# A decoder layer on one core: eight triangular matrices inverted together instead of four and four

## The chip, the cores and the metric

The kernel runs on one core of a Trainium2 chip. The core has TensorE (matrix products, with a queue that loads weights ahead), VectorE (DVE), ScalarE (ACT), GpSimd (POOL) and SyncE (SP, which issues most of the transfers). The metric is the device time of one run in microseconds; lower is better.

## The reference

One layer of a decoder with 256 positions of 1024 features. A norm is followed by one projection whose columns go to two mixers:

- softmax attention with 8 heads of 64 (one block, a relative bias, normed queries and keys), with a gate;
- a gated delta rule with 4 heads of 128. Queries, keys and values pass a convolution of width 4. The 256 positions of a head are cut into chunks of 64, and in each chunk a lower triangular system is solved:

```
g = cumsum(g, axis=-1)                       # per chunk of 64
decay = where(incl, exp(g_i - g_j), 0)
lmat = where(strict, (k*beta) @ k.T * decay, 0);  amat = lmat + eye(C)
u = triangular_solve(amat, v * beta)
w = triangular_solve(amat, k * beta * exp(g))
def step(state, xs):                         # over the chunks
    v_new = u_i - w_i @ state
    o_i = q_i @ state + a_i @ v_new
    state = state * gl_i + k_i.T @ v_new
```

Both outputs are gated, joined, projected back to 1024 and added to the input.

## The kernel before, in words

**Large products.** The weights stream in as chunks of 512 KB (8 smaller `z`, 12 `d`, 16 `a`, 8 `o`). Each is split into a high part (`wh`, a cast on ScalarE, L195) and the rest (`wl`, a subtraction on VectorE, L196), and every product runs as three products of 256 columns (L256 to L258, L747 to L749, L836 to L838). The `z` chunks give the gates, `d` the queries, keys and values of the delta rule, `a` those of the attention and its gate, `o` is the output projection.

**The order.** `products()` emits the large products in steps of six and yields after each; `advance()` then counts a slot (`now`) and lets every other stream (`bias`, `norm`, `gates`, `prep`, `base`, `scan`, `heads`, `pair`) whose slot has come emit its next step. The table `AT` gives the slot of each step of each stream; a slot that has passed means the next one. If `products()` itself must wait (for the bank of PSUM or, in the output projection, for a head that isn't done), slots go by without a large product. TensorE runs in exactly the order in which its instructions are emitted. The other engines' order is set by a planner at build time, which lets what is ready go ahead of what was emitted earlier, with streams preferred to the splits of weights.

**The delta rule.** The kernel uses chunks of 128, two for each head, so 8 triangular matrices (index `u`). `prep(0)` makes those of heads 0 and 1, `prep(2)` those of heads 2 and 3: transposes of keys and queries (L438), products of them (L462), then the scaled triangle `LT` (L466) and transposes of values (L478). `base` inverts: the 16x16 blocks on the diagonal by substitution on VectorE, 15 steps of a multiply (L507) and a subtraction (L509), then `levels` puts them together to 32, 64 and 128 with small products on 32- or 64-row tiles of TensorE (L529; L535 and L537; L552; L558 to L560; L568; L574), with an eviction to SBUF after each. The result is `MT`. `scan` then runs the chunks of a head in five dependent steps (L589; L595 and L596; L610 and L611; L618; L622), norms the output with a power on GpSimd, transposes it (L634) and writes `yh` and `yl`, high part and rest (L635, L636). `scan` of head 2 waits for head 0 and that of head 3 for head 1.

Before, `base(0)` with `levels(0)` does the four matrices of heads 0 and 1 as soon as `prep(0)` has them, and `base(1)` those of heads 2 and 3 after `prep(2)`; each set of levels uses one bank.

**Attention.** `heads4` norms and transposes queries and keys (L663); `pair` does two heads: logits (L689), softmax on VectorE and ScalarE (L696, L123, L700, L707), transposes (L712), product with the values (L723, L725).

**Output.** `OUTS` orders the output chunks. The second chunk needs heads 0 and 1 of the scan, the fifth needs attention heads 4 to 7, the seventh needs scan heads 2 and 3.

**Others that move.** `bias` has one product (L381) whose result is copied (L384) and sent through memory to spread the relative bias. `norm` ends with L297, whose copy (`rbc`) each convolution (L403, L405, L407) reads. `gates` makes the decays: its small steps end with `g` (L345), which L352, L353 and L363 read.

Of the kernel before, what the change touches and what calls it, by code (L numbers as in the profile page):

```python
# [11 lines left out]
ALU = mybir.AluOpType  # L12
AX = mybir.AxisListType

P = 128
# [5 lines left out]
DH = 4  # L21
# [6 lines left out]
C_ID, C_MN, C_U, C_ND = range(4)  # L28
# [6 lines left out]
LD, LS, PRI, REP, MTL, BDK = 7, 4, 100, 16, 1, 14  # L35
OUTS = ((0, 2), (0, 0), (1, 2), (1, 0), (0, 3), (1, 3), (0, 1), (1, 1))
AT = {
    ("attention", 0): 88, ("attention", 1): 97, ("attention", 2): 128, ("attention", 3): 117, ("attention", 4): 120,
# [3 lines left out]
    ("base1", 8): 124, ("bias", 0): 0, ("bias", 1): 6, ("bias", 2): 43, ("gates", 0): 29, ("gates", 1): 35,  # L42
# [13 lines left out]
}  # L56
SEGS = (2, 0, 1, 3)
W_NORM, W_BA, W_PREP, W_BASE, W_LV, W_SC, W_Y, W_QK, W_SM, W_PT, W_HD, NP = 7, 16, 4, 34, 2, 3, 5, 6, 2, 2, 3, 2
# [3 lines left out]
def tile_hymba_layer(ctx: ExitStack, tc: tile.TileContext, xt, wz, wdn, wat, wout, rb, cst, oneh, out):  # L62
# [11 lines left out]
    def new(shape, name, dt=F32):  # L74
        return cp.tile(shape, dt, name=name, tag=name)
# [20 lines left out]
    def start(name, gen, wait=1):  # L96
        streams.append([gen, AT.get((name, 0), now[0] + wait), name, 0])
# [137 lines left out]
    cvd = new([P, DH, 2], "cvd")  # L235
    M = new([64, 8, 64], "M")
    MT = new([P, 8, P], "MT")
    Mts = [new([P, 4, 32], f"Mt{g}") for g in range(2)]
    for t in (M, MT):
        POOL.memset(t, 0.0)  # L240

    def basis():
        for t in Mts:
            nc.gpsimd.dma_start(t, cst[:, C_ND, :])

    if not MTL:
        basis()
# [175 lines left out]
    def prep(hp, n, ps):  # L423
# [60 lines left out]

    def base(gq):
        us = slice(4 * gq, 4 * gq + 4)
        pk = rot([P, 16, 4], f"pk{gq}", "pk")
        for q in range(4):  # L490
            r = slice(32 * q, 32 * q + 32)

            DVE.scalar_tensor_tensor(out=pk[r].rearrange("p i u -> p u i"), in0=LT[r, us, 32 * q + 16:32 * q + 32],
                                     scalar=cs2[r, 0:1], in1=LT[r, us, 32 * q:32 * q + 16], op0=ALU.mult, op1=ALU.add)
        Lb = rot([P, 16, 32], f"Lb{gq}", "Lb", 1)
        DVE.transpose(Lb, pk.unsqueeze(3).to_broadcast([P, 16, 4, 8]))
        Mt = Mts[gq]
        tm = rot([P, 4, 16], f"tm{gq}", "tm")
# [12 lines left out]
        Mp = rot([P, 4, 4, 8], f"Mp{gq}", "Mp")  # L511
        DVE.transpose(Mp.rearrange("p u c g -> p c u g"), Mt)
        Mp = Mp.rearrange("p u c g -> p u (c g)")
        for q in range(4):
            r = slice(32 * q, 32 * q + 32)
            DVE.transpose(MT[r, us, r], Mp[r])
        yield W_BASE
        yield from levels(gq, Mp)


    def levels(gq, Mp):
        us = slice(4 * gq, 4 * gq + 4)
        uu = range(4 * gq, 4 * gq + 4)
        b = yield from grab()
        b32 = b.rearrange("p (z u i) -> p z u i", z=4, i=32)
# [4 lines left out]
        X16 = rot([P, 4, 16], f"X16{gq}", "X16")  # L530
        ACT.mul(X16, b32[:, 2, :, 0:16], cs2[:, 0:1])
        yield W_LV
        for i, u in enumerate(uu):
            for q, r in enumerate(qs):
                PE.matmul(b32[r, 3, i, 0:16], lhsT=MT[r, u, r], rhs=X16[r, i, :], start=True, stop=True)  # L535
            for q, r in enumerate(qs):
                PE.matmul(b32[32 * q:32 * q + 16, 3, i, 16:32], lhsT=X16[r, i, :], rhs=MT[r, u, 32 * q + 16:32 * q + 32],  # L537
                          start=True, stop=True)
        DVE.tensor_tensor(out=Mp[:, :, 0:16], in0=Mp[:, :, 0:16], in1=b32[:, 3, :, 0:16], op=ALU.subtract)
        for q in range(4):  # L540
            r = slice(32 * q, 32 * q + 16)
            o = MT[r, us, 32 * q + 16:32 * q + 32]
            if q % 2:
                ACT.mul(o, b32[r, 3, :, 16:32], -1.0)
            else:
                DVE.tensor_scalar(out=o, in0=b32[r, 3, :, 16:32], scalar1=-1.0, scalar2=None, op0=ALU.mult)
        for q in range(2):
            POOL.tensor_copy(M[qs[q], us, qs[q]], Mp[qs[q]])
        yield W_LV
        for i, u in enumerate(uu):  # L550
            for r, c in ((q0, q1), (q2, q3)):
                PE.matmul(b32[c, 0, i, :], lhsT=LT[r, u, c], rhs=Mp[r, i, :], start=True, stop=True)  # L552
        X32 = rot([P, 4, 32], f"X32{gq}", "X32")
        ACT.copy(X32[q1], b32[q1, 0])
        DVE.tensor_copy(X32[q3], b32[q3, 0])
        yield W_LV
        for i, u in enumerate(uu):
            PE.matmul(b32[q1, 1, i, :], lhsT=MT[q1, u, q1], rhs=X32[q1, i, :], start=True, stop=True)  # L558
            PE.matmul(b32[q2, 1, i, :], lhsT=X32[q3, i, :], rhs=MT[q3, u, q3], start=True, stop=True)
            PE.matmul(b32[q0, 1, i, :], lhsT=X32[q1, i, :], rhs=MT[q1, u, q1], start=True, stop=True)  # L560
        DVE.tensor_scalar(out=M[q1, us, q0], in0=b32[q1, 1], scalar1=-1.0, scalar2=None, op0=ALU.mult)
        ACT.mul(MT[q2, us, q3], b32[q2, 1], -1.0)
        ACT.mul(MT[q0, us, q1], b32[q0, 1], -1.0)
        yield W_LV
        b64 = b.rearrange("p (z u i) -> p z u i", z=2, i=64)
        for i, u in enumerate(uu):
            for c in (q2, q3):
                PE.matmul(b64[c, 1, i, :], lhsT=LT[0:64, u, c], rhs=M[:, u, :], start=True, stop=True)  # L568
        X64 = rot([P, 4, 64], f"X64{gq}", "k2", 4)
        ACT.copy(X64[64:128], b64[64:128, 1])  # L570
        yield W_LV
        for i, u in enumerate(uu):
            for c, o in ((q0, 0), (q1, 32)):
                PE.matmul(b64[c, 0, i, :], lhsT=X64[64:128, i, o:o + 32], rhs=MT[64:128, u, 64:128], start=True, stop=True)  # L574
# [361 lines left out]
```

## Time and profile before

| | us |
|---|---|
| median of 3 runs (lowest, highest) | 165.27 (165.08, 165.45) |
| the profiled execution | 166.0 |
| its span, first to last instruction | 164.1 |
| TensorE busy in the span | 156.8 (96%) |
| VectorE busy | 130.3 (79%) |
| ScalarE busy | 103.1 (63%) |
| GpSimd busy | 19.8 (12%) |

The profile is of one execution. A product of TensorE has one or two records (a float32 product of two passes has two). Products overlap, so a busy TensorE is read by the time from the start of one to the start of the next. "Idle before" is what the engine stood still ahead of an instruction, with the instruction that it waited for.

### The profile page before, as it was taken

Reading aid. Unit: us, or ns where it says so; the run is one execution under the profiler, and the core shown is the slowest. Engines: PE = TensorE matmul, PEld = TensorE weight load, DVE = VectorE, ACT = ScalarE, POOL = GpSimd, SP = SyncE. Lnnn points to the kernel's source line nnn. Section 1 sums busy time; section 2 is a strip of 40 time slices with the busy share of each in tenths; the row PEclk is TensorE's granted clock in tenths of the full one; section 3 lists DMA queues with packets and bytes.
Section 4 is the critical chain, followed back from the end, with each engine's and each line's share of the span. In section 5 each row is a group of like instructions: output and inputs, shape, how many; then the busy total and the mean of one; then the engine's idle time right before and its main releaser. Section 6 shows DMA issues by size and latency. Waiting matters only on the chain.

```text
span 164.1 us, 4034 instructions
## 1 busy us (share of the span) xinstructions
PE 156.8 (96%) x1548; PEld 148.3 (90%) x1548; DVE 130.3 (79%) x381; ACT 103.1 (63%) x244; POOL 19.8 (12%) x29
## 2 busy tenths in 40 slices
PE   7999899999999999999999999999999979999990
PEld 7869899999999999999999989989988858999990
DVE  2569859999598999999999999987676997356261
ACT  5769497539988558787636695655657885343100
POOL 7200410000002000031230001042220010003000
PEclk9999999999999999999999999999999999999999
DMA  5999888899965327574344434434312300000033
GB/s 148 270 365 355 248 262 222 248 179 192 339 206 209 128 80 213 223 216 172 122 138 135 132 123 134 128 132 132 116 51 93 128 0 4 0 0 0 4 128 128
DMA packets 9930, 25.01 MB, mean 152 GB/s; under 512 B 1165, under 2 KB 3981, under 8 KB 9912
## 3 DMA queue, kind: packets, MB, share of 16 engines
q1 hardware_dynamic: 9208, 23.66, 46.6%
q10 hardware_dynamic: 576, 0.92, 1.5%
q8 instruction: 12, 0.20, 0.5%
q0 software_dynamic: 128, 0.18, 0.4%
q14 instruction: 6, 0.05, 0.1%
HBM read 23.52 MB, written 1.25 MB: 151 GB/s over the span
## 4 chain that ended last, share of the span: by engine, by line
PE 70%; DVE 13%; ACT 6%; DMA 3%; issue 2%; SPq 2%; POOL 1%; DVEq 0%
PE ps L256 8%; PE ps L257 7%; PE ps L258 7%; PE ps L748 6%; PE ps L749 6%; PE ps L747 6%; PE ps L836 4%; PE ps L838 4%; PE ps L837 4%; DVE wl_d L196 3%; DMA px<-xt 3%; PE ps L462 2%; DVE cv L407 2%; PE ps L689 1%; PE ps L712 1%
## 5 line engine op out<-in xcount | busy, mean ns | idle before, releaser
L256 PE MATMUL ps<-wh_a,xh 128*128 128x256 f32 x96 | 28.5, 297 | 0.0
L747 PE MATMUL ps<-xh,wh_d 128*128 128x256 f32 x96 | 27.8, 289 | 0.0
L748 PE MATMUL ps<-xl,wh_d 128*128 128x256 f32 x96 | 26.8, 280 | 0.0
L749 PE MATMUL ps<-xh,wl_d 128*128 128x256 f32 x96 | 26.8, 279 | 0.0
L257 PE MATMUL ps<-wh_a,xl 128*128 128x256 f32 x96 | 26.7, 279 | 0.0
L258 PE MATMUL ps<-wl_a,xh 128*128 128x256 f32 x96 | 26.7, 279 | 0.0
L195 ACT CAST wh_a<-wr_a 128x1024 fp32r<-128x1024 f32 x16 | 16.8, 1049 | 7.2 <-PE ps L748 3.7
L196 DVE TENSOR_TENSOR wl_a<-wr_a,wh_a 128x1024 fp32r<-128x1024 f32 x16 | 19.4, 1215 | 0.7 <-ACT wh_a L195 0.6
L256 PEld LDWEIGHTS ps<-wh_a,xh 128*128 128x128 f32 x96 | 18.1, 188 | 0.7 <-issue 0.5
L836 PE MATMUL ps<-yh,wh_o 128*128 128x256 f32 x64 | 18.7, 292 | 0.0
L257 PEld LDWEIGHTS ps<-wh_a,xl 128*128 128x128 f32 x96 | 18.1, 188 | 0.1
L258 PEld LDWEIGHTS ps<-wl_a,xh 128*128 128x128 f32 x96 | 18.1, 189 | 0.0
L748 PEld LDWEIGHTS ps<-xl,wh_d 128*128 128x128 f32 x96 | 18.1, 188 | 0.1
L747 PEld LDWEIGHTS ps<-xh,wh_d 128*128 128x128 f32 x96 | 18.0, 188 | 0.1
L407 DVE SCALAR_TENSOR_TENSOR cv<-un,px,cv 128x255 f32<-128x255 f32 (+2 forms) x36 | 16.4, 475 | 2.0 <-ACT cv L405 2.0
L749 PEld LDWEIGHTS ps<-xh,wl_d 128*128 128x128 f32 x96 | 18.0, 187 | 0.0
L837 PE MATMUL ps<-yl,wh_o 128*128 128x256 f32 x64 | 17.9, 280 | 0.0
L838 PE MATMUL ps<-yh,wl_o 128*128 128x256 f32 x64 | 17.9, 279 | 0.0
L196 DVE TENSOR_TENSOR wl_d<-wr_d,wh_d 128x1024 fp32r<-128x1024 f32 x12 | 14.6, 1214 | 1.2 <-ACT wh_d L195 1.1
L195 ACT CAST wh_d<-wr_d 128x1024 fp32r<-128x1024 f32 x12 | 12.6, 1052 | 2.4 <-PE ps L748 1.9
L196 DVE TENSOR_TENSOR wl_o<-wr_o,wh_o 128x1024 fp32r<-128x1024 f32 x8 | 9.8, 1221 | 3.6 <-ACT wh_o L195 3.6
L836 PEld LDWEIGHTS ps<-yh,wh_o 128*128 128x128 f32 x64 | 12.0, 188 | 0.5 <-issue 0.3
(210 smaller groups left out, 406.7 us busy)
## 6 DMA issues: line engine op xcount, KB each, us to landing
wr_a<-wat SPq DMA_DIRECT2D x16, 512.0 KB, 3.3
wr_d<-wdn SPq DMA_DIRECT2D x12, 512.0 KB, 5.6
wr_o<-wout SPq DMA_DIRECT2D x8, 512.0 KB, 3.3
wr_z<-wz SPq DMA_DIRECT2D x7, 260.0 KB, 5.8
T<-bd SPq DMA_DIRECT2D x8, 128.0 KB, 5.8
px<-xt SPq DMA_DIRECT2D x7, 128.0 KB, 4.9
out_t<-ot ACTq DMA_DIRECT2D x3, 256.0 KB, 2.4
cs<-cst SPq DMA_DIRECT2D x1, 192.0 KB, 4.9
```

What stands on the lines that cost most here:

```text
L195: ACT.copy(h[:, r], raw[:, r])
L196: eng.tensor_tensor(out=l[:, r], in0=raw[:, r], in1=h[:, r].bitcast(F32), op=ALU.subtract)
L256: PE.matmul(ps, lhsT=xa, rhs=wh[:, cols], start=first, stop=False)
L257: PE.matmul(ps, lhsT=xb, rhs=wh[:, cols], start=False, stop=False)
L258: PE.matmul(ps, lhsT=xa, rhs=wl[:, cols], start=False, stop=last)
L407: DVE.scalar_tensor_tensor(out=a[:, 3 - j:], in0=src[:, 0:S - 3 + j], scalar=pr[:, o + j:o + j + 1], in1=a[:, 3 - j:], op0=ALU.mult, op1=A ...
L747: PE.matmul(ps, lhsT=w[0][:, wk], rhs=xh[:, k, :], start=first, stop=False)
L748: PE.matmul(ps, lhsT=w[0][:, wk], rhs=xl[:, k, :], start=False, stop=False)
L749: PE.matmul(ps, lhsT=w[1][:, wk], rhs=xh[:, k, :], start=False, stop=last)
L836: PE.matmul(ps, lhsT=w[0][:, o], rhs=yh[:, k, :], start=(first and j == 0 and (m % 2 == 0 or alone)), stop=False)
L837: PE.matmul(ps, lhsT=w[0][:, o], rhs=yl[:, k, :], start=False, stop=False)
L838: PE.matmul(ps, lhsT=w[1][:, o], rhs=yh[:, k, :], start=False, stop=(last and j == 1 and (m % 2 == 1 or alone)))
```

## The change

All eight matrices are inverted in one `base`, started when `prep(2)` has its triangles, with instructions twice as wide, and one pass of `levels` over eight matrices with two banks; the last eviction is shared by VectorE and ScalarE. All four `scan` streams are then started at once (2 and 3 still wait for 0 and 1). The slots of all streams are set anew.

```diff
 AT = {
-    ("base0", 0): 40, ("base0", 1): 100, ("base0", 2): 107, ("base0", 3): 112, ("base0", 4): 105, ("base0", 5): 116,
-    ("base0", 6): 104, ("base0", 7): 107, ("base0", 8): 119, ("base1", 0): 93, ("base1", 1): 117, ("base1", 2): 107,
-    ("base1", 3): 121, ("base1", 4): 125, ("base1", 5): 118, ("base1", 6): 116, ("base1", 7): 122,
-    ("base1", 8): 124, ("bias", 0): 0, ("bias", 1): 6, ("bias", 2): 43, ("gates", 0): 29, ("gates", 1): 35,
-    ("gates", 2): 29, ("gates", 3): 49, ("heads00", 0): 82, ("heads00", 1): 96, ("heads01", 0): 120,
-    ("heads01", 1): 120, ("heads10", 0): 95, ("heads10", 1): 98, ("heads11", 0): 125, ("heads11", 1): 127,
-    ("norm", 0): 13, ("norm", 1): 14, ("norm", 2): 18, ("pair0", 0): 101, ("pair0", 1): 112, ("pair0", 2): 118,
-    ("pair1", 0): 93, ("pair1", 1): 107, ("pair1", 2): 118, ("pair2", 0): 111, ("pair2", 1): 148, ("pair2", 2): 151,
-    ("pair3", 0): 144, ("pair3", 1): 187, ("pair3", 2): 193, ("prep0", 0): 44, ("prep0", 1): 30, ("prep0", 2): 46,
...
+    ("attention", 0): 17, ("attention", 1): 45, ("attention", 2): 15, ("attention", 3): 5, ("attention", 4): 38,
+    ("base", 0): 15, ("base", 1): 121, ("base", 2): 127, ("base", 3): 128, ("base", 4): 129, ("base", 5): 130,
+    ("base", 6): 131, ("bias", 0): 15, ("bias", 1): 20, ("bias", 2): 49, ("gates", 0): 27, ("gates", 1): 27,
+    ("gates", 2): 29, ("gates", 3): 30, ("heads00", 0): 11, ("heads00", 1): 92, ("heads01", 0): 35,
+    ("heads01", 1): 121, ("heads10", 0): 14, ("heads10", 1): 102, ("heads11", 0): 1, ("heads11", 1): 128,
+    ("norm", 0): 7, ("norm", 1): 14, ("norm", 2): 28, ("pair0", 0): 105, ("pair0", 1): 120, ("pair0", 2): 121,
+    ("pair1", 0): 105, ("pair1", 1): 120, ("pair1", 2): 121, ("pair2", 0): 130, ("pair2", 1): 134,
+    ("pair2", 2): 138, ("pair3", 0): 136, ("pair3", 1): 140, ("pair3", 2): 142, ("prep0", 0): 53, ("prep0", 1): 54,
+    ("prep0", 2): 55, ("prep0", 3): 36, ("prep0", 4): 58, ("prep0", 5): 59, ("prep0", 6): 60, ("prep0", 7): 61,
+    ("prep0", 8): 38, ("prep2", 0): 30, ("prep2", 1): 67, ("prep2", 2): 76, ("prep2", 3): 15, ("prep2", 4): 78,
+    ("prep2", 5): 79, ("prep2", 6): 80, ("prep2", 7): 81, ("prep2", 8): 24, ("scan0", 0): 132, ("scan0", 1): 133,
+    ("scan0", 2): 134, ("scan0", 3): 136, ("scan0", 4): 134, ("scan0", 5): 140, ("scan1", 0): 132,
+    ("scan1", 1): 133, ("scan1", 2): 134, ("scan1", 3): 136, ("scan1", 4): 137, ("scan1", 5): 142,
+    ("scan2", 0): 141, ("scan2", 1): 143, ("scan2", 2): 144, ("scan2", 3): 147, ("scan2", 4): 147,
+    ("scan2", 5): 159, ("scan3", 0): 142, ("scan3", 1): 143, ("scan3", 2): 144, ("scan3", 3): 147,
+    ("scan3", 4): 148, ("scan3", 5): 157,
 }
...
-    Mts = [new([P, 4, 32], f"Mt{g}") for g in range(2)]
+    Mt = new([P, 320], "Mt")
...
-        start(f"base{hp // 2}", base(hp // 2))
+        if hp == 2:
+            start("base", base())
...
-    def base(gq):
+    def base():
...
-            t = ap(tm, 0, (32, 2), (16, nc_), (1, w))
-            m = ap(Mt, r + 1, (80, 2), (32, nc_), (1, w))
-            SUB.tensor_tensor(out=t, in0=ap(Lb, 32 * (r + 1) + r, (16, 2), (0, nc_), (32, w)),
-                               in1=ap(Mt, r, (80, 2), (32, nc_), (0, w)), op=ALU.mult)
+            t = ap(tm, 0, (32, 4), (16, nc_), (1, w))
+            m = ap(Mt, r + 1, (80, 4), (32, nc_), (1, w))
+            SUB.tensor_tensor(out=t, in0=ap(Lb, 64 * (r + 1) + r, (16, 4), (0, nc_), (64, w)),
+                              in1=ap(Mt, r, (80, 4), (32, nc_), (0, w)), op=ALU.mult)
             SUB.tensor_tensor(out=m, in0=m, in1=t, op=ALU.subtract)
...
-    def levels(gq, Mp):
-        us = slice(4 * gq, 4 * gq + 4)
-        uu = range(4 * gq, 4 * gq + 4)
-        b = yield from grab()
+    def levels(Mp):
+        while len(free) <= keep[0] + 1:
+            yield
+        ba, bb = free.pop(0), free.pop(0)
...
-        for i, u in enumerate(uu):
+        for u in range(8):
             for r in qs:
-                PE.matmul(b32[r, 2, i, 0:16], lhsT=LT[r, u, r], rhs=Mp[r, i, 0:16], start=True, stop=True)
+                PE.matmul(a32[r, 0, u, 0:16], lhsT=LT[r, u, r], rhs=Mp[r, u, 0:16], start=True, stop=True)
...
-        ACT.mul(MT[0:64, us, 64:128], b64[0:64, 0], -1.0)
-        free.append(b)
-        yield W_LV
-        start(f"scan{2 * gq}", scan(2 * gq))
-        yield 1
-        start(f"scan{2 * gq + 1}", scan(2 * gq + 1))
+        DVE.tensor_scalar(out=MT[0:64, 0:4, 64:128], in0=b64[0:64, 0:4], scalar1=-1.0, scalar2=None, op0=ALU.mult)
+        ACT.mul(MT[0:64, 4:8, 64:128], b64[0:64, 4:8], -1.0)
+        free.extend((ba, bb))
+        for h in range(DH):
+            start(f"scan{h}", scan(h))
```

## Rows read from the trace of the kernel before

**Rows 1.** Windows: length, busy us of PE, PEld, DVE, ACT, POOL; granted clock; transfers.

```profile
18.00:125.00 107.00, 106.86 (x1174) 102.45 (x1173) 95.04 (x280) 73.02 (x176) 13.68 (x14) 1.00 0.57 171
...
128.90:137.80 8.90, 7.73 (x61) 5.66 (x59) 8.14 (x34) 7.14 (x22) 0.69 (x1) 1.00 0.15 52
137.80:160.00 22.20, 22.20 (x190) 22.08 (x188) 11.26 (x31) 5.79 (x12) 1.36 (x2) 1.00 0.07 25
```

**Rows 2.** The waits of TensorE's weight loads: us in total, times, longest.

```profile
PEld ps L712 <- DVE pb L707: 1.9, 3, 1.1
```

**Rows 3.** Groups by line: count, busy us, mean ns of one, idle before.

```profile
L507 DVE TENSOR_TENSOR tm<-Lb,Mt 128x28 f32<-128x28 f32 (+10 forms) x30 | 5.5, 184 | 0.4
L509 DVE TENSOR_TENSOR Mt<-Mt,tm 128x28 f32<-128x28 f32 (+10 forms) x30 | 5.3, 175 | 0.5
...
L635 ACT ACTIVATE yh<-ps,px 128x256 fp32r<-128x256 f32 x4 | 1.9, 469 | 3.5 <-PE ps L634 3.5
...
L636 DVE SCALAR_TENSOR_TENSOR yl<-ps,px,yh 128x256 fp32r<-128x256 f32 x4 | 1.9, 482 | 2.4 <-ACT yh L635 2.4
```

**Rows 4.** TensorE in order of time, around two stages of levels: start, us.

```profile
88.78 0.28 PE L258 MATMUL ps<-wl_a,xh 128*128 128x256 f32 x1
88.99 0.44 PE L529 MATMUL ps<-Mp,LT 32*32 32x16 f32 x32
89.36 0.39 PE L256 MATMUL ps<-wh_a,xh 128*128 128x256 f32 x1
89.58 0.28 PE L257 MATMUL ps<-wh_a,xl 128*128 128x256 f32 x1
...
107.95 0.44 PE L529 MATMUL ps<-Mp,LT 32*32 32x16 f32 x32
108.32 0.39 PE L256 MATMUL ps<-wh_a,xh 128*128 128x256 f32 x1
```

**Rows 5.** TensorE in order of time, around the bias product.

```profile
10.18 0.29 PE L258 MATMUL ps<-wl_z,xh 128*128 128x264 f32 x1
10.40 0.81 PE L381 MATMUL ps<-T,rbt 33*8 33x384 f32 x2
...
11.36 0.36 PE L257 MATMUL ps<-wh_z,xl 128*128 128x256 f32 x1
11.95 0.39 PE L258 MATMUL ps<-wl_z,xh 128*128 128x256 f32 x1 [0.23 <-DVE wl_z L196]
```

**Rows 6.** TensorE in order of time: the norm's broadcast and the first gate product.

```profile
21.00 0.60 PE L297 MATMUL ps<-cs,rtok 128*128 128x128 f32 x4
...
33.47 0.28 PE L352 MATMUL ps<-g,cs 128*128 128x8 f32 x2
```

**Rows 7.** VectorE in order of time: the end of the gate steps.

```profile
30.55 0.16 DVE L345 TENSOR_TENSOR g<-ln,eal 128x8 f32<-128x8 f32 x1
```

**Rows 8.** The chain that ended last, from 124 to 140 us: start, us, what.

```profile
124.99 0.91 PE ps L689 x8
...
130.60 1.13 DVE wl_o L196
...
136.17 0.22 PE ps L610 x2
...
137.06 0.58 PE ps L723 x4
137.64 0.22 PE ps L725 x4
```

**Rows 9.** TensorE in order of time, in the stretch without large products.

```profile
129.69 0.93 PE L689 MATMUL ps<-kT,qT 64*128 64x128 f32 x8
...
134.68 0.81 PE L712 MATMUL ps<-cs,pb 128*128 128x128 f32 x4 [0.91 <-DVE pb L707]
135.73 0.44 PE L712 MATMUL ps<-cs,pb 128*128 128x128 f32 x2 [0.24 <-DVE pb L707]
...
137.79 0.39 PE L836 MATMUL ps<-yh,wh_o 128*128 128x256 f32 x1
```

More of the change, by code (lines that the diff above doesn't have):

```diff
@@ L242, in basis @@
     def basis():
-        for t in Mts:
-            nc.gpsimd.dma_start(t, cst[:, C_ND, :])
+        for g in range(2):
+            nc.gpsimd.dma_start(Mt[:, 160 * g:160 * g + P], cst[:, C_ND, :])
     if not MTL:
@@ L482, in prep @@
             yield 1
-    def base(gq):
-        us = slice(4 * gq, 4 * gq + 4)
-        pk = rot([P, 16, 4], f"pk{gq}", "pk")
+    def base():
+        pk = rot([P, 16, 8], "pk", "pk", 1)
         for q in range(4):
             r = slice(32 * q, 32 * q + 32)
[L493 to L498, printed above, removed]
+            DVE.scalar_tensor_tensor(out=pk[r].rearrange("p i u -> p u i"), in0=LT[r, :, 32 * q + 16:32 * q + 32],
+                                     scalar=cs2[r, 0:1], in1=LT[r, :, 32 * q:32 * q + 16], op0=ALU.mult, op1=ALU.add)
+        Lb = rot([P, 16, 64], "Lb", "Lb", 1)
+        DVE.transpose(Lb, pk.unsqueeze(3).to_broadcast([P, 16, 8, 8]))
+        tm = rot([P, 8, 16], "tm", "tm", 1)
         def ap(t, offset, *dims):
@@ L515, in base @@
             r = slice(32 * q, 32 * q + 32)
-            DVE.transpose(MT[r, us, r], Mp[r])
+            DVE.transpose(MT[r, :, r], Mp[r])
         yield W_BASE
-        yield from levels(gq, Mp)
-    def levels(gq, Mp):
-        us = slice(4 * gq, 4 * gq + 4)
-        uu = range(4 * gq, 4 * gq + 4)
-        b = yield from grab()
-        b32 = b.rearrange("p (z u i) -> p z u i", z=4, i=32)
+        yield from levels(Mp)
+    def levels(Mp):
+        while len(free) <= keep[0] + 1:
+            yield
+        ba, bb = free.pop(0), free.pop(0)
@@ L532, in levels @@
+        X16 = rot([P, 8, 16], "X16", "X16", 1)
+        ACT.mul(X16, a32[:, 0, :, 0:16], cs2[:, 0:1])
         yield W_LV
-        for i, u in enumerate(uu):
+        for u in range(8):
+            for r in qs:
+                PE.matmul(a32[r, 1, u, 0:16], lhsT=MT[r, u, r], rhs=X16[r, u, :], start=True, stop=True)
             for q, r in enumerate(qs):
-                PE.matmul(b32[r, 3, i, 0:16], lhsT=MT[r, u, r], rhs=X16[r, i, :], start=True, stop=True)
-            for q, r in enumerate(qs):
-                PE.matmul(b32[32 * q:32 * q + 16, 3, i, 16:32], lhsT=X16[r, i, :], rhs=MT[r, u, 32 * q + 16:32 * q + 32],
+                PE.matmul(a32[32 * q:32 * q + 16, 1, u, 16:32], lhsT=X16[r, u, :], rhs=MT[r, u, 32 * q + 16:32 * q + 32],
@@ L538, in levels @@
                           start=True, stop=True)
-        DVE.tensor_tensor(out=Mp[:, :, 0:16], in0=Mp[:, :, 0:16], in1=b32[:, 3, :, 0:16], op=ALU.subtract)
+        DVE.tensor_tensor(out=Mp[:, :, 0:16], in0=Mp[:, :, 0:16], in1=a32[:, 1, :, 0:16], op=ALU.subtract)
         for q in range(4):
             r = slice(32 * q, 32 * q + 16)
-            o = MT[r, us, 32 * q + 16:32 * q + 32]
+            o = MT[r, :, 32 * q + 16:32 * q + 32]
             if q % 2:
-                ACT.mul(o, b32[r, 3, :, 16:32], -1.0)
+                ACT.mul(o, a32[r, 1, :, 16:32], -1.0)
@@ L545, in levels @@
             else:
-                DVE.tensor_scalar(out=o, in0=b32[r, 3, :, 16:32], scalar1=-1.0, scalar2=None, op0=ALU.mult)
+                DVE.tensor_scalar(out=o, in0=a32[r, 1, :, 16:32], scalar1=-1.0, scalar2=None, op0=ALU.mult)
         for q in range(2):
-            POOL.tensor_copy(M[qs[q], us, qs[q]], Mp[qs[q]])
+            POOL.tensor_copy(M[qs[q], :, qs[q]], Mp[qs[q]])
         yield W_LV
-        for i, u in enumerate(uu):
+        for u in range(8):
             for r, c in ((q0, q1), (q2, q3)):
-                PE.matmul(b32[c, 0, i, :], lhsT=LT[r, u, c], rhs=Mp[r, i, :], start=True, stop=True)
@@ L553, in levels @@
-        X32 = rot([P, 4, 32], f"X32{gq}", "X32")
+                PE.matmul(b32[c, 0, u, :], lhsT=LT[r, u, c], rhs=Mp[r, u, :], start=True, stop=True)
+        X32 = rot([P, 8, 32], "X32", "X32", 1)
         ACT.copy(X32[q1], b32[q1, 0])
@@ L556, in levels @@
         yield W_LV
[L557 to L562, printed above, removed]
@@ L563, in levels @@
-        ACT.mul(MT[q0, us, q1], b32[q0, 1], -1.0)
+        for u in range(8):
+            PE.matmul(b32[q1, 1, u, :], lhsT=MT[q1, u, q1], rhs=X32[q1, u, :], start=True, stop=True)
+            PE.matmul(b32[q2, 1, u, :], lhsT=X32[q3, u, :], rhs=MT[q3, u, q3], start=True, stop=True)
+            PE.matmul(b32[q0, 1, u, :], lhsT=X32[q1, u, :], rhs=MT[q1, u, q1], start=True, stop=True)
+        DVE.tensor_scalar(out=M[q1, :, q0], in0=b32[q1, 1], scalar1=-1.0, scalar2=None, op0=ALU.mult)
+        ACT.mul(MT[q2, :, q3], b32[q2, 1], -1.0)
@@ L564, in levels @@
+        ACT.mul(MT[q0, :, q1], b32[q0, 1], -1.0)
         yield W_LV
-        b64 = b.rearrange("p (z u i) -> p z u i", z=2, i=64)
-        for i, u in enumerate(uu):
+        a64, b64 = (b.rearrange("p (u i) -> p u i", i=64) for b in (ba, bb))
+        for u in range(8):
             for c in (q2, q3):
-                PE.matmul(b64[c, 1, i, :], lhsT=LT[0:64, u, c], rhs=M[:, u, :], start=True, stop=True)
-        X64 = rot([P, 4, 64], f"X64{gq}", "k2", 4)
-        ACT.copy(X64[64:128], b64[64:128, 1])
+                PE.matmul(a64[c, u, :], lhsT=LT[0:64, u, c], rhs=M[:, u, :], start=True, stop=True)
@@ L571, in levels @@
+        X64 = rot([P, 8, 64], "X64", "k2", 4)
+        ACT.copy(X64[64:128], a64[64:128])
         yield W_LV
-        for i, u in enumerate(uu):
+        for u in range(8):
             for c, o in ((q0, 0), (q1, 32)):
-                PE.matmul(b64[c, 0, i, :], lhsT=X64[64:128, i, o:o + 32], rhs=MT[64:128, u, 64:128], start=True, stop=True)
-        ACT.mul(MT[0:64, us, 64:128], b64[0:64, 0], -1.0)
-        free.append(b)
-        yield W_LV
-        start(f"scan{2 * gq}", scan(2 * gq))
-        yield 1
```

11 lines of the change are left out of this document (6 added, 5 removed), and 8 rows, old and new, of the table AT.

## The prediction

> **What bounds the kernel now.** I read the windows first. From 18 to 125 us TensorE is busy for 106.86 of 107.00 us, and from 137.8 us to the end of its work for all of 22.20; between them lies a stretch of 8.9 us in which it works for 7.73 [rows 1]. So almost nothing is left idle: the order of TensorE's instructions is written out by hand through the slots, TensorE runs through it without a gap, and its own work sets the end. VectorE is busy for 95.04 of the same 107.00 us and ScalarE for 73.02, but neither holds TensorE up there. The waits say the same: the transposes of the softmax weights (L712) waited three times, 1.9 us in sum, for the VectorE step ahead of them (L707) [rows 2]; two of the three lie in the stretch of 8.9 us. A change to this kernel therefore counts by three things only: how long TensorE's own instructions take, what is put into its dense stretches, and how long it stands still where the order leaves it no large product to do. Work taken from VectorE or ScalarE counts for nothing by itself.
>
> **Part 1: half the substitution instructions.** Before, 30 multiplies (L507, mean 184 ns) and 30 subtractions (L509, mean 175 ns) [rows 3] are 5.5 + 5.3 = 10.8 us of VectorE. After, 15 + 15 of twice the width. A width of 128x28 costs little more than the smallest ones in these groups, so I take 200 to 250 ns for each, 6 to 7.5 us in all. The packing, the transposes and the evictions halve in number too. VectorE saves 5 to 6 us and TensorE nothing, since in the dense stretch [rows 1] it does not wait for VectorE. In the slot table the one substitution starts at slot 81 and its first product (L529) is due at slot 121: 40 slots of about 0.7 us, which covers the 7 us several times.
>
> **Part 2: one pass of levels.** The number of small products is the same (168, two records each). What changes is how often TensorE goes over from large products to 32- or 64-row tiles and back. The rows show the price [rows 4]: a large product follows the one before by 0.12 us, the first small one starts 0.21 us after the last large one (88.78 to 88.99), the 32 records take 0.37 us, and the second large product starts 0.22 us after the first (89.36 to 89.58). So each visit costs 0.09 + 0.10 = 0.19 us beside its content. Where one small stage follows another, as at 107.95, the second adds its 0.37 us alone. I count visits by walking the two slot tables, each slot's stream steps in order and then one step of large products. Before, up to the stretch at 128.9 us, 13: slots 100, 101, 107, 112, 113, 116, 117, 118, 121, 125, 126, 127, 129. After, 7: slots 105, 121 and 127 to 131. Six fewer at 0.19 us: **-1.1 us**. If VectorE's wider evictions made the stages wait, that is under part 4.
>
> **Part 3: the early slots.** The bias product (L381) moves from the first slots, due from slot 6, to slot 20. Where it stands it is free: after it, a product waits at 11.95 us for a split weight (idle 0.23 us shown) that came from the input's load, and without L381 TensorE would only have waited longer [rows 5]. At slot 20 it stands among the first d products, where TensorE has no gap. Its price is 11.36 - 10.18 = 1.18 us less the two steps of 0.12 that the large products would take: **+0.9 us**. The bound below is 0, if TensorE afterwards waits for something that doesn't move.
>
> The broadcast of the norm (L297) moves from slot 18 to 28, and with it the first convolution step (L403), which reads it. L297 ran at 21.00 us [rows 6]; ten slots at 0.71 us (six products of 0.12) and L381 later is about 29 us, so the convolutions can begin 8 us later than they could before. The gate product (L352) ran at 33.47 us in slot 35 [rows 6] and now stands in slot 28, right after L297, at about 29.5 us. It needs g (L345), which VectorE finished at 30.71 us before [rows 7]. Before, VectorE put convolution steps in between the small gate steps that lead to g; these can't run now until L297 has, so I take it that g comes in time. If it comes at 30.71 us as before, L352 stands 1.2 us, and all that TensorE has left stands behind it. The later convolutions feed L438 of head 3, which moves from slot 79 to 76. I take **+0.2 us** for all these, between 0 and +1.5.
>
> **Part 4: a chain with less cover.** In the new table the level stages stand at slots 127, 128, 129, 130 and 131, one step of large products (0.7 us) between each two, and scan 0 and 1 start at 132. Each stage's eviction (0.25 to 0.5 us, and some 0.2 us from product to eviction) fits under 0.7 us if the evicting engine is free; behind a weight split on VectorE (1.13 us [rows 8]) it doesn't. Also the softmax of pair 2 starts at slot 130. I take **+0.3 us**, between 0 and +1.
>
> Then comes the stretch without large products, slots 133 to 142, as the output products of the first half need scan 0 and 1. Its content: scan steps 1 to 4 of two heads at once, pair 2, all of pair 3, the last step of heads 0 and 1 and the first of 2 and 3. A product of 128 columns takes 0.22 us in two records [rows 8]. In sum: L595/596 0.88, six transposes L712 0.65, L610/611 0.88, L689 1.05 (0.91 and a part of a visit), L618 0.44, L622 0.44, L723/725 0.8 (0.58 + 0.22), L712 0.65, then 0.44, 0.8 and 0.44: 7.5 us. The wait in it: pair 3's L689 started at 129.69 us before, its transposes at 134.68, the last of them at 135.73 (0.91 and 0.24 us of shown idle) and the large products resumed at 137.79 [rows 9]. So 6.3 us passed from L689 to the end of L712. After, TensorE has only L618, L622 and L723/725 to do in that time, 1.05 + 0.44 + 0.44 + 0.8 = 2.7 us with L689 itself, and then L712's own 0.65. With the latency of before that is 2.9 us of standing still; if VectorE is freer (before, pair 2's L707 and a weight split of 1.13 us [rows 8] stood ahead of pair 3's) 5.1 us pass and 1.7 us remain. Behind it, scan 1's last step now stands right before the large products that read its result: a copy (L635, 469 ns) and a subtraction (L636, 482 ns) [rows 3], of which 0.3 to 0.5 us stay uncovered; another 0.3 us for the second copy of pair 3's transposes. Together 2.35 to 3.55 us. Before, the stretch took 8.9 us for 6.5 us of content by the same prices: 2.4 us. The difference is -0.1 to +1.2, and **+0.6 us** is what I take.
>
> **What goes.** The third wait of L712 was in slot 107, for a softmax started 6 slots earlier; it is now started 15 slots earlier. 1.9 less 1.1 and about 0.4 for the other two, and what else of small waits goes in the dense part: **-0.4 us** (0 to -0.7).
>
> Sum: -1.1 + 0.9 + 0.2 + 0.3 + 0.6 - 0.4 = +0.5 us. The profiled execution took 166.0 us (164.1 of span and 1.9 around it); so 166.5 for one like it, and 165.27 + 0.5 = 165.8 us for the median of runs.
>
> **The rivals.**
> - *Faster: the visits go and nothing comes for them.* If L381 is absorbed by a wait after it, or the stretch without large products waits no longer than before, -1.1 - 0.4 + 0.3 and one of the two positive terms remain: -0.3 to -1.2 us, 164.1 to 165.0. It speaks for it that VectorE is 5 us freer and that 1.13 us of weight split stood in pair 3's way; against it that L381's new neighbours are dense. It decides as soon as pair 3's L712 ends within 5 us of its L689.
> - *Nothing to measure.* The terms are small and of both signs; with the stretch at its lower end and L381 paid in full the sum is -0.2 to +0.2: 165.1 to 165.5.
> - *Much slower: the early chain.* If g comes at 30.7 us as before, L352 stands 1.2 us; if the convolutions, up to 8 us later, reach L438 of head 3 late, another 1 to 2 us; and all level stages wait behind splits, 1 us. Then +2 to +3: 167.3 to 168.3.
> - *The clock.* In the stretch of waits the granted clock was 1.00 throughout [rows 1], with TensorE still for 0.91 us at the longest. That is the higher of its two levels, 2.4 GHz. Were longer waits to bring the lower one (1.2 GHz) for the first two steps of large products behind them, each of these 12 would cost 0.12 us more: 1.4 us, and with the +0.5, 167.2 us. The Trainium skill (TensorE: Matmul & The Clock Gate, section "Why this matters for your kernels") warns of that: idle gaps between bursts put the engine back to half clock. By that rule, the trace agrees for a gap of 0.91 us that it is too short for it; longer ones no run here shows.
>
> **How the numbers follow.** The forecast (slower by 0.3 to 1.3 us) 0.41; faster 0.33; nothing to measure 0.21; the early chain 0.04 and the clock 0.01, slower both. 0.2% (0.33 us) is about what a measurement of this kernel can tell from no change. Slower is 0.46. The range leaves out a tenth at each end: 164.2, near the floor of the faster case, and 167.6, inside the early-chain case. The likeliest case alone is 165.6 to 166.6.
>
> **What would show it.** Right: about six fewer visits, levels in one group from L529 to L574, the first L381 among d products with dense neighbours, idle ahead of pair 3's L712 of over 1.2 us, and TensorE's work summing to 0.2 us less. Wrong: idle ahead of L352 or L438; level stages that wait; L712 of pair 3 without a wait; or a stage of 64 records that takes more than twice one of 32.

## The result, and the profile after

The changed kernel takes 166.57 us (median of 4 runs, 166.38 to 167.35), the kernel before beside it 165.18 (164.74 to 165.45): a ratio of 1.0091, 95% interval 1.0064 to 1.0117, or +1.1 to +1.9 us. The forecast was slower by 0.5 us, with 0.3 to 1.3 as its own range. Executions that take over 1.5% longer than the fastest of their kernel count as slow and are left out of every ratio (times in us are medians of all), which matters for one run only, the old work in the new slots, where three of six are left out.

The profiled execution of the kernel before (166.0 us) was a long one of its kind, by a late transfer, as a second profile of it shows below (span 163.5 where the first had 164.1). Of after the profiled one is the shortest of the four (166.38, span 164.6), 0.2 us under their median. So the account is made between the second profile of before and that of after. The lines of the kernel after have slightly other numbers: the bias product L381 is L379 there, L478 is L477, L663 is L662, L712 is L711, and L529 to L574 are the same.

First the windows after (busy time and records of each engine, then the granted clock, the DMA share and GB/s), which answer to [rows 1]:

```profile
72.00:88.00 16.00, 15.18 (x131) 14.93 (x130) 14.95 (x38) 8.68 (x14) 4.18 (x2) 1.00 0.43 142
88.00:104.00 16.00, 16.00 (x142) 15.50 (x141) 15.03 (x56) 11.12 (x26) 0.00 (x0) 1.00 0.46 156
104.00:112.00 8.00, 7.87 (x131) 7.18 (x130) 6.33 (x14) 4.71 (x10) 2.58 (x2) 1.00 0.50 152
112.00:126.00 14.00, 13.10 (x340) 11.69 (x339) 8.85 (x26) 7.94 (x21) 2.52 (x3) 1.00 0.31 106
126.00:138.00 12.00, 10.68 (x78) 7.97 (x77) 9.84 (x43) 8.77 (x29) 1.45 (x2) 1.00 0.00 0
```

TensorE, without a gap here before, now loses 0.8 us in the first window and 0.9 in the fourth. VectorE is busy for 14.95 of 16.00 and 15.03 of 16.00 us in the first two: nearly full. The prediction read from such windows that VectorE holds nothing up, and did not ask how late it may be. The waits of TensorE after name the places; they answer to [rows 2]:

```profile
PE ps L552 <- issue: 0.9, 1, 0.9
PE ps L662 <- DVE qn L654: 0.8, 1, 0.8
PE ps L621 <- ACT v L619: 0.8, 2, 0.5
PE ps L711 <- DVE pb L706: 0.5, 2, 0.3
```

The last two stand in the stretch without large products. The first two are new. TensorE in order of time at both, after:

```profile
81.58 0.28 PE L748 MATMUL ps<-xh,wl_a 128*128 128x256 f32 x1
82.67 0.66 PE L662 MATMUL ps<-cs,qn 128*128 128x128 f32 x4 [0.82 <-DVE qn L654]
...
115.20 0.22 PE L537 MATMUL ps<-MT,X 32*16 32x16 f32 x6
116.25 0.56 PE L552 MATMUL ps<-Mp,LT 32*32 32x32 f32 x23
117.72 0.32 PE L552 MATMUL ps<-Mp,LT 32*32 32x32 f32 x9 [0.90 <-issue]
```

At L662 the normalised q is late. VectorE's and GpSimd's rows show why: the wide transpose of the substitution (L495, 1.24 us) stands ahead of the small step L649, which releases the GpSimd power, that power takes 2.55 us (1.63 at this place in the second profile of before), and VectorE itself waits for it:

```profile
77.98 1.24 DVE L495 STREAM_TRANSPOSE Lb<-pk 128x1024 f32<-128x1024 f32 x1
79.14 0.13 DVE L649 SCALAR_TENSOR_TENSOR s<-s,emt 128x8 f32<-128x8 f32 x1
...
81.93 0.69 DVE L654 TENSOR_TENSOR qn<-ps,r 128x512 f32<-128x512 f32 x1 [0.81 <-POOL r L133]
```

```profile
79.35 2.55 POOL L133 TENSOR_TENSOR r<-s,mhalf 128x8 f32<-128x8 f32 x1 [8.69 <-DVE s L649]
```

L552 pauses after 23 of its 32 records, with its operands there and no wait that the profile shows. The substitution answers to [rows 3]: 15 + 15 instructions, 6.2 us where 60 took 10.8.

```profile
L505 DVE TENSOR_TENSOR tm<-Lb,Mt 128x56 f32<-128x56 f32 (+10 forms) x15 | 3.3, 218 | 0.2
L507 DVE TENSOR_TENSOR Mt<-Mt,tm 128x56 f32<-128x56 f32 (+10 forms) x15 | 2.9, 195 | 0.2
```

**The account**, from 20 us on: the cost of a group of small products is the time from the last large product ahead of it to the second one behind it, less two spacings of 0.118 us, summed by stage for both traces.

| | before (second profile) | after | forecast |
|---|---|---|---|
| bias product among the d products | 0 | +0.93 | +0.9 |
| norm and gates (L297, L352 to L363) | 3.08 | 2.67: -0.4 | +0.2 |
| `prep` (L438, L462, L478) | 6.39 | 6.11: -0.3 | in the next |
| small products from the levels on, without standing still | 25.6 | 23.8: -1.8 | -1.5 |
| L662 of the first two heads | 0.88 | 1.90: +1.0 | 0 |
| pause in L552 | 0 | +0.9 | 0 (+0.3 for waits of levels) |
| standing still without large products | 2.5 | 3.6: +1.1 | +0.6 |

The standing still is what the stretch takes beyond the content that the prediction priced (6.5 and 7.5 us): 8.97 and 11.06 us, the latter with 0.55 us of gaps inside the first output products behind it. It is more than the waits that the trace lists there (1.2 us before, 1.3 after), since behind a wait or a change of shape records follow each other by 0.2 to 0.3 us, not by the priced 0.11. The sum is +1.4. The last large product starts 1.3 us later than in before (160.50 against 159.22).

### The profile page after: what moved, and what is told of

Its sections match the earlier page's. It is cut to its first block, busy times and chain, and to the rows that moved or that the text cites. A ratio compares the mean times of both kernels' runs of the same rounds, so it can differ in the third digit from the quotient of the medians.

```text
span 164.6 us, 3986 instructions
## 1 busy us (share of the span) xinstructions
PE 155.2 (94%) x1548; PEld 147.2 (89%) x1548; DVE 126.3 (77%) x338; ACT 101.5 (62%) x236; POOL 20.0 (12%) x27
## 4 chain that ended last, share of the span: by engine, by line
PE 67%; DVE 17%; ACT 4%; issue 4%; POOL 3%; DMA 2%; SPq 0%; DVEq 0%; POOLq 0%; ACTq 0%
PE ps L746 9%; PE ps L747 9%; PE ps L748 9%; PE ps L835 5%; PE ps L836 5%; PE ps L837 4%; PE ps L256 4%; PE ps L254 4%; PE ps L255 4%; DVE wl_a L194 4%; POOL r L133 3%; DMA wr_z<-wz 2%; DVE pb L706 2%; PE ps L688 2%; PE ps L662 1%
## 5 line engine op out<-in xcount | busy, mean ns | idle before, releaser
L254 PE MATMUL ps<-wh_a,xh 128*128 128x256 f32 x96 | 27.8, 289 | 0.0
L193 ACT CAST wh_a<-wr_a 128x1024 fp32r<-128x1024 f32 x16 | 16.9, 1053 | 10.8 <-PE ps L255 5.6
L133 POOL TENSOR_TENSOR r<-s,mhalf 128x8 f32<-128x8 f32 x4 | 8.5, 2127 | 34.6 <-DVE s L649 34.6
```

What stands on the lines that cost most here:

```text
L193: ACT.copy(h[:, r], raw[:, r])
L254: PE.matmul(ps, lhsT=xa, rhs=wh[:, cols], start=first, stop=False)
```

## The experiments

Each ratio is to the kernel before, run beside it on the same chip.

**Before again.** No edit.

> The kernel before, unchanged, for a second profile: the profiled execution behind the prediction took 166.0 us where its median is 165.1. Theory: the difference lies in waits for transfers ahead of the first products or for the z weights (before 21 us), and the second trace has the same order and the same waits from there on. Rival: it lies in the stages around the inversion, so that the sum of the prediction rests on a stage that is usually shorter.

165.44 us. The first d product started at 20.30 us in the first profile; here, and then after:

```profile
19.73 0.28 PE L747 MATMUL ps<-xh,wh_d 128*128 128x256 f32 x1
```

```profile
19.66 0.28 PE L746 MATMUL ps<-xh,wh_d 128*128 128x256 f32 x1
```

From there on the two traces of before keep a distance of 0.56 to 0.60 us to the end: the same order and waits (L712 waits 1.2 us in both). The theory holds. It also settles that L381 costs nothing where it stands before: that kernel has it in its first slots and starts the d products at the same time as the changed kernel, which has not. The wait that absorbs it is not the one at 11.95 us [rows 5] but a later one, for the sums of squares of the norm (`sq`, L285, ready at 16.9 us here): without L381 ahead of it TensorE stands 0.64 us for them in the changed kernel and 0.54 us in the next run, with it not at all. In the first profile `sq` came 0.6 us later, behind a transfer of the input for which ScalarE waited 1.40 us; that is the 0.64 us that one could read from it.

**The bias product alone**, in the kernel before:

```diff
-    ("bias", 0): 0, ("bias", 1): 6,
+    ("bias", 0): 15, ("bias", 1): 20,
```

> The kernel before with one thing of the change alone: the sums over the stop columns (L381) and the steps around them start at the slots that the change gives them (15 and 20 where before has 0 and 6). Theory of the prediction: in their old place the products cost nothing, because TensorE waited there for transfers anyway, and at slot 20 they cost 0.93 us; the ratio to before is 1.0056 (+0.9 us). Rival, from the trace after the change, whose first large product starts at 19.66 us against 20.30 before: the old place cost some 0.64 us too, so that +0.3 us is left, a ratio of 1.002.

167.37 us, 1.0122 (1.0087 to 1.0157): +1.4 to +2.6, more than either expected. The product costs 0.93 us in its new place, as the theory says. The rest appears at 90 us, at the first level:

```profile
90.20 0.44 PE L529 MATMUL ps<-Mp,LT 32*32 32x16 f32 x32 [0.86 <-DVE Mp L512]
```

In both traces of before this L529 follows its large product without a wait. The planner had put VectorE's instructions in another order: by line and tile, 26 of the 381 stand elsewhere, many of them convolution steps between 25 and 65 us. The inverted blocks are there at 90.1 us, where the second profile of before has them at 87.6 and its L529 at 88.4. So in the kernel before the substitution meets its slot with less than 1 us to spare.

**The transposes of the first head later**, in the changed kernel:

```diff
-("heads00", 1): 92
+("heads00", 1): 96
```

> The changed kernel with the wide transposes of the first head (L662) four slots later, 96 where the change has 92. Theory: the wait of 0.82 us ahead of them at 82.67 us in the trace after the change (for the normalised q of L654, which stands behind a GpSimd power of 2.55 us) goes, and the time is 0.8 to 1.0 us under that of the changed kernel: a ratio to before of about 1.004 where the changed kernel has 1.009. Rival: the wait was cover for something that now waits later, or TensorE is late there anyway, and the ratio stays at 1.008 to 1.010.

167.67 us, 1.0150 (1.0103 to 1.0196): not faster. VectorE's order hardly moved here (one of 338 instructions). The wait of 0.82 us is gone at its old place and comes back longer at the next transposes that need a normalised q, and the pause is longer too:

```profile
PE ps L662 <- DVE qn L654: 1.4, 1, 1.4
PE ps L552 <- issue: 1.2, 1, 1.2
```

The rival holds: TensorE came there 1.2 us earlier (the large product ahead of the group started at 105.64 us instead of 106.83), but VectorE's L654 started at 108.66 us here and at 108.60 in the changed kernel. That point is set by VectorE and GpSimd, and what TensorE gains ahead of it is lost at it.

**The levels two slots apart**, in the changed kernel:

```diff
-    ("base", 2): 127, ("base", 3): 128, ("base", 4): 129, ("base", 5): 130,
+    ("base", 2): 123, ("base", 3): 125, ("base", 4): 127, ("base", 5): 129,
```

> The changed kernel with the levels of the inversion two slots apart (121, 123, 125, 127, 129 where the change has 121, 127, 128, 129, 130), so that they stand between large products one by one. Theory: the pause of 0.90 us inside the records of L552 comes from the dense run of tiny products ahead of it (128 of the second level directly behind one another and 32 more), and it goes; one more visit to the small tiles costs 0.2 us; the ratio to before falls from 1.009 to about 1.005. Rival: the pause does not hang on the neighbours and stays, and the ratio is 1.010.

168.44 us, 1.0177 (1.0136 to 1.0217). Half of the theory holds: L552 runs in one piece (x32 at 116.00). But new waits take more than the pause:

```profile
PE ps L558 <- DVE X L555: 1.7, 1, 1.7
PE ps L552 <- DVE Mp L539: 0.5, 1, 0.5
```

VectorE has the copies that a level needs behind a qn that waits for GpSimd (L654) and behind a weight split of 1.23 us, which itself waits 1.41 us for ScalarE's high part.

**The second level alone two slots earlier**, in the changed kernel:

```diff
-    ("base", 2): 127,
+    ("base", 2): 125,
```

> The changed kernel with the second level (L535, L537) two slots earlier, 125 where the change has 127, so that its 128 tiny products and the 32 of the third level (L552, slot 128) have three slots of large products between them instead of one. Theory: the pause of 0.90 us in L552, which no wait explains and which was gone with the levels two slots apart, comes from the tiny products standing close together; it goes, and since the third level stays where it is, VectorE's waits of that run do not come: the ratio falls from 1.009 to 1.003 to 1.005. Rival: the pause is cover for the levels after it (their operands pass ScalarE and VectorE), which then wait, and the ratio stays at 1.008 to 1.011.

165.80 us, 1.0016 (0.998 to 1.0053): the most that one slot gave back, some 1.2 us. The theory holds; VectorE's order is that of the changed kernel. L552 runs in one piece, its group 1.21 us where the changed kernel pays 2.29:

```profile
118.67 0.28 PE L748 MATMUL ps<-xh,wl_a 128*128 128x256 f32 x1
118.88 0.69 PE L552 MATMUL ps<-Mp,LT 32*32 32x32 f32 x32
```

The profiled execution was the longest of this kernel's runs (167.9, with late z weights and 1.1 us of waiting for kq at 52 us), so it shows the place, and the median the gain.

**The new slots with the old work**, two sets of four:

```diff
-    def base():
-        pk = rot([P, 16, 8], "pk", "pk", 1)
+    def base(gq):
+        us = slice(4 * gq, 4 * gq + 4)
+        pk = rot([P, 16, 4], f"pk{gq}", "pk")
```

> The slots of the changed kernel, but the work of the kernel before: two sets of four matrices, VectorE's substitution in 60 instructions of half the width, and two passes of levels with one bank each, both sets' levels in the same slots. Theory: TensorE sees the same order of products and the same visits, and the 4 us that the wide substitution saves VectorE lie under large products in both, so the time is that of the changed kernel within 0.4 us (ratio to before 1.007 to 1.011): the slots alone make the difference. Rival: the wide form itself matters, and the ratio is above 1.013 (the shorter substitution was needed) or below 1.005 (the wide levels cost something).

1.0408 (1.0356 to 1.0459), or 171.3 to 172.5 us, against both. The rival holds, in the direction that speaks for the wide form: in these slots the shorter substitution and evictions together are worth some 5 us; the run does not split them. Without them ScalarE and VectorE fall behind (kq late for 2.2 us at 69 us, and 1.0 us inside the levels), and the profiled execution (175.5 us) then has the lower clock from 125.5 to 135.8 us:

```profile
PE ps L437 <- ACT kq L122: 2.6, 2, 2.2
PE ps L567 <- ACT MT L562: 1.0, 1, 1.0
```

```profile
124.00:126.00 2.00, 0.64 (x16) 0.53 (x17) 1.30 (x3) 0.83 (x4) 0.00 (x0) 0.89 0.33 66
126.00:128.00 2.00, 1.99 (x22) 1.76 (x24) 0.00 (x0) 0.67 (x2) 0.00 (x0) 0.50 0.54 205
```

**The bias product back in its early slots**, in the changed kernel:

```diff
-("bias", 0): 15, ("bias", 1): 20
+("bias", 0): 0, ("bias", 1): 6
```

> The changed kernel with the sums over the stop columns (L379) back in the slots that they have before (0 and 6 instead of 15 and 20): the counterpart of the run that moves them alone in the kernel before, where it cost 2.3 us. Theory: the ratio falls from 1.009 to 1.003 or less, since the 0.3 to 0.6 us of TensorE come with what they push back on VectorE. Rival: with the wide substitution VectorE has 4 us of slack there, and only the 0.3 us of the z stage come back: 1.007.

178.15 us, 1.0779 (1.0728 to 1.0830). Both theories fall. From 22 us on TensorE is 1.0 us earlier, but VectorE's order is another one (25 of 338 instructions stand elsewhere, most of them between 48 and 61 us), and vc is late for L477:

```profile
60.60 0.44 PE L477 MATMUL ps<-cs,vc 128*128 128x128 f32 x2 [4.02 <-ACT vc L121]
```

Another 7.7 us come between 121 and 152 us, 0.8 of them a wait of L568 for VectorE, the rest by the clock above all: from the pause in L552 (0.85 us, ending at 122.99) to 139.9 us it is 0.50, the lower level of 1.2 GHz, and large products follow each other by 0.21 us instead of 0.12:

```profile
126.00:128.00 2.00, 2.00 (x48) 1.94 (x42) 1.78 (x3) 1.19 (x2) 0.00 (x0) 0.50 0.02 4
138.00:140.00 2.00, 2.00 (x12) 2.00 (x11) 0.70 (x2) 1.12 (x3) 0.00 (x0) 0.52 0.00 0
```

The changed kernel keeps 1.00 in the same stretch behind nearly the same pause. Why one falls and the other does not stays open.

**The inversion earlier, so that no slot lacks large products**, 43 slots of the changed kernel, the first of them:

```diff
-    ("base", 1): 121, ("base", 2): 127, ("base", 3): 128,
+    ("base", 1): 106, ("base", 2): 108, ("base", 3): 111,
```

> The changed kernel with 43 other slots: the six levels of the wide inversion at 106, 108, 111, 113, 116, 118 instead of 121, 127 to 131, so that both scans and the four pairs fit between large products, and no slot is left without them. Theory: the stretch without large products costs some 3.6 us of standing still, the waits at L662 and in L552 1.7 us more; three more visits cost 0.6 us, and waits of levels on VectorE behind a split (1.2 us in the run with the levels two slots apart) cost 1 to 2; the ratio to before is 0.98 to 0.995. Rival: VectorE is what sets the time from 60 us on, a wait that goes in one place comes back in another, and the ratio stays above 1.003.

172.76 us, 1.0454 (1.0402 to 1.0507). I had taken slots for even steps of time; slot 106 comes at 94 us, and VectorE has the inverted blocks at about 100:

```profile
100.01 1.05 PE L529 MATMUL ps<-Mp,LT 32*32 32x16 f32 x64 [6.09 <-DVE Mp L511]
100.99 0.58 PE L254 MATMUL ps<-wh_a,xh 128*128 128x256 f32 x1
101.37 0.41 PE L255 MATMUL ps<-wh_a,xl 128*128 128x256 f32 x1
101.59 0.41 PE L256 MATMUL ps<-wl_a,xh 128*128 128x256 f32 x1
```

Standing for 6.09 us brought the lower clock as well (0.50 from 97.6 to 104.4 us). So the wide inversion can't start at slot 106: one pass gives nothing until all eight matrices are substituted, at 100 us here and 103.5 in the changed kernel. There its first level comes at 107.0 us; a start in the 3.5 us between was not run.

**The same, three slots apart** (106, 109, 112, 115, 118, 121, with the scans three slots later).

> As the run with the inversion under large products, but its levels three slots apart (106, 109, 112, 115, 118, 121). Theory: a slot is 0.93 us, a level's way over ScalarE or VectorE with a split ahead of it takes up to 2.5 us, so three slots cover it where two don't: 0.5 to 1.5 us faster than the other, if its levels wait at all. Rival: the scans, three slots later, leave the first products of the output waiting, and it is slower by 0.5 to 1 us.

178.27 us, 1.0798 (1.0744 to 1.0852). L529 waits 6.1 us here too. No later level waits for an operand in either of the two runs, so a third slot had nothing to cover. The rival holds, and by more than its 1 us: from 139 us on L633 and the first output products, which need the scans, wait 2.7 us in sum (0.9 in the other run), and behind that the clock is at 0.50 a second time, from 142.6 to 149.4 us.

**Without the GpSimd power in the heads**, in the changed kernel and in the kernel before:

```diff
-        r8 = rot([P, 8], f"r8{seg}{hf}", "r8")
-        rsqrt(r8, s8)
...
-                          in1=r8.unsqueeze(2)
+                          in1=s8.unsqueeze(2)
```

> The changed kernel without the GpSimd power in the attention heads: q and k are multiplied by the mean square itself instead of its inverse root, which leaves out the normalisation and nothing of the other engines' work. Theory: VectorE stands still for 0.81, 1.53 and 1.19 us for these powers, and TensorE 0.82 us behind the first (L662); without them VectorE is 2 to 3.5 us earlier at the levels, L662 waits for nothing, and the time falls by 1 to 2 us, to a ratio of 0.997 to 1.003. Rival: VectorE has slack there, only the wait at L662 goes or not even that, and the ratio stays above 1.004.

> The same left out of the kernel before. Theory: there VectorE waits once for such a power, 1.07 us at 111 us, and TensorE behind none of them, so that the time falls by 0 to 0.5 us (0.997 to 1.0). Rival: VectorE sets the pace there as well, and it falls by 1 us or more.

166.52 us, 1.0050 (1.0013 to 1.0088), and 166.53, 1.0059 (1.0030 to 1.0088). In the changed kernel L662 no longer waits and some 0.7 us come back, less than the theory wants. But the clock has a part in that: the traced execution, with the pause in L552 at 1.09 us, is at 0.50 from 118.2 to 121.6 us (0.99 over its span). Five of the twelve executions are at 0.99 or less; the other seven, at 0.996 or more like the changed kernel's own, have a median of 165.62 us, a ratio of 1.0013, and there some 1.3 us come back, as the theory has it. In before leaving work out costs 1 us: 13 of 381 VectorE instructions stand elsewhere, and L529 waits 0.5 us for Mp. So leaving the power out brings about 1 us in the changed kernel, with 17 of 338 VectorE instructions elsewhere as well; in before the new order hides what it is worth.

**Three slots moved together**: the second level at 125, L662 at 96 and its third head at 124.

> The changed kernel with three other slots: the second level at 125 as in the run that cured the pause in L552, the transposes of the first head (L662) at 96, and those of the third at 124 instead of 121, so that the wait of 1.38 us which took the place of the first one has somewhere to be covered. Theory: the waits for the normalised q and k are worth 0.8 us once neither has TensorE behind it; with the pause gone the ratio to before is 0.995 to 0.999, faster than both kernels. Rival: the planner puts VectorE's instructions in another order whenever such a step moves, and what that brings is as large as what goes: the ratio is 1.002 or more.

166.06 us, 1.0036 (1.0008 to 1.0065). By the ratio the rival holds, though not for its reason: one VectorE instruction stands elsewhere. The pause is gone, but the wait for qn is there for the third time, now at a large product, whose bank of PSUM this L654 has still to read:

```profile
PE ps L746 <- DVE qn L654: 1.4, 1, 1.4
```

VectorE's L654 starts at 109.50 us here, 0.9 later than in the changed kernel. No version beat the kernel before.

## Why the prediction was right in its direction and short in size

**The sum.** The measured +1.4 us (+1.1 to +1.9) lies at the upper end of the 0.3 to 1.3 of the forecast case, and inside the range. That the direction came true is luck in part. The terms that the prediction names come to -0.5 us by the account (+0.9 - 0.4 - 0.3 - 1.8 + 1.1), which is its *faster* rival; what makes the kernel slower is the wait at L662 (+1.0) and the pause in L552 (+0.9), and neither was in the sum. Two runs bear this out: without the pause the ratio is 1.0016, without the wait for the power 1.0013 where the clock stays up. TensorE's own work, for which the sign was 0.2 us less, fell by 1.6.

**Visits (-1.1, small waits -0.4).** Right for the visits: 13 before and 7 after, as counted, the level stages stand in one group from L529 to L574, and a stage of 64 records takes no more than twice one of 32. The account has -1.8 there and -0.3 in `prep`; six visits at 0.19 us are 1.1 of it, and what makes up the rest was not taken apart. The small waits were misread: [rows 2] are waits of the weight loads, and TensorE itself stood still for L707 only twice in the first profile, both times in the stretch without large products:

```profile
PE ps L712 <- DVE pb L707: 1.2, 2, 0.9
```

**L381 (+0.9).** Right: 0.93 in both kernels that have it at slot 20, and free in its old place, though by a later wait than the one named.

**Early slots (+0.2).** Wrong in sign, small: no wait at L352 or L438; the gates' second group lost a stall and cost 0.89 instead of 1.30. The early-chain rival is out.

**The chain of levels (+0.3).** The named mechanism, evictions behind splits, did not come in the changed kernel; its levels wait for no operand. It came in the run with the levels two slots apart, at 2.2 us. In its place stood the pause in L552, +0.9, which the prediction did not see; that it fits the range of 0 to +1 is luck. It is shown to hang on the closeness of the stages: 0.85 to 1.16 us after 23 or 24 records in all four kernels with the wide levels 2 and 3 in neighbouring slots (the changed one, the first head's transposes later, the bias early, no power), and none in the five where they stand two or more slots apart. The Trainium skill (Runtime: NRT & Kernel Launch, section "Instruction fetch mechanics") has instructions arrive in blocks by a queue of the engine's own, at a cost that is mostly hidden. The traces bear on it: one queue of instructions moves 16 KB twelve times in each run, about once for every 128 of TensorE's 1548 records, so I take it for TensorE's.

```profile
q8 instruction: 12, 0.20, 0.5%
```

In all four kernels the pause ends at the same place of the program (record 1118, in one of them 1119), 1.30 to 1.44 us after such a transfer has ended (116.32 us in the changed kernel, the pause 117.72). In the two runs with the second level at slot 125 that record comes 1.6 us after the transfer, and nothing waits. The 128 records up to there take 2.2 us in the changed kernel and 3.5 with the second level earlier; large products take 15 us for as many. So the pause is most likely a wait for the next block; no run changes the fetch alone, and that step is argued.

**The stretch without large products (+0.6).** Right in the main, mis-sized: 3.6 us of standing still against 2.5 before, so +1.1 (the prediction's own parts add up to 2.3 to 3.7 us, not to 2.35 to 3.55). Pair 3 takes 5.7 us from L688 to the end of L711, between its 5.1 and 6.3, for 3.35 us of work. But its sign, over 1.2 us of idle ahead of that L711, did not come: these are 0.5 us. Another 0.8 stand ahead of L621, for ScalarE's v in the scans, which it does not name, and 0.55 us pass inside the first output products. The stretch costs 10.5 us in the runs with L662 later and with the second level earlier as well, so those two changed nothing there.

**The step that failed** is "Work taken from VectorE or ScalarE counts for nothing by itself". It was read from TensorE's dense windows [rows 1], where nothing waits; but that VectorE has idle time there (95.04 of 107.00 us busy) does not say how late a single result may be. The run with only the bias product moved lost 0.86 us at Mp, the old work in the new slots lost 5 us, and the new wait at L662 (+1.0) is VectorE's and GpSimd's as well. The saving was needed in the new slots; it bought no time over before.

**The clock** was weighed at 0.01 and plays no part in the result (1.00 from 7 us to the last product in the profiles of both kernels), but the neighbours of this kernel fall into it: the runs at 172 and 178 us, and some executions of the one without the power. The Trainium skill (TensorE: Matmul & The Clock Gate, section "Why this matters for your kernels") warns of half clock after idle gaps; the traces agree for 4.02 and 6.09 us, and show it in three runs inside a stretch of short waits and small products as well (the bias early, the old work, no power), where the prediction's row of 0.91 us [rows 9] had none.

## What to carry to other kernels

An engine with no gap sets the end only as long as the others deliver in time: read how full the second engine is in the same windows before its work is counted as free, since a slot moved ahead of a late operand only moves the wait. When a pass is made wide to save fixed costs, ask when its first result comes: half the matrices at 88 us had cover for all of their chain, all eight at 103 had none left for the scans. Small products that follow each other by the hundred can run into a pause that no operand explains; large ones put between them cured it here. Where the order of the other engines is planned anew at each build, judge an edit by how much of that order it changes: here none or one instruction in some, 13 to 26 in others.

## What the hardware showed that was not expected

- TensorE paused for 0.85 to 1.16 us inside a run of 32 independent small products, 1.0 us behind 128 others, with no wait on record, and went on 1.30 to 1.44 us after a 16 KB transfer of an instruction queue had ended.
- The granted clock fell to 0.50 in the stretch of levels and scans behind idle times of at most 1.1 us each: for 17 us with the bias early, 10 us with the old work in the new slots, 3 us without the power; and not in the changed kernel behind 0.90, nor with L662 later behind 1.16.
- The same GpSimd power on 128x8 took 2.55, 1.63, 2.48 and 1.85 us in one execution.
